# Splitting the opening load of a prefix-sum kernel between two DMA queues

## The chip, the core and the metric

The kernel runs on one core of one Trainium2 chip. Five engines work side by side, each with its own instruction stream: TensorE (PE, matrix products), VectorE (DVE), ScalarE (ACT), GpSimd (POOL) and SyncE (SP). Data comes from the device memory (HBM) into the on-chip SBUF of 128 partitions by DMA. Three of the engines issue DMAs here: SP and ACT into hardware queues, POOL into a software queue that can also convert float32 to bfloat16 on the way. All queues are served by the core's 16 DMA engines.

The metric is device time in microseconds (us); less is better. Beside it stands the profile of one execution, whose span is the time between its first and last instruction.

## The reference

The input x has 4 batches of 4224 x 4224 float32 numbers. For each batch the reference takes the two-dimensional prefix sum, reads its diagonal, and sums that up once more:

```
ps = np.cumsum(np.cumsum(x, axis=1), axis=2)
diag = np.diagonal(ps, axis1=1, axis2=2)
return np.cumsum(diag, axis=1).astype(np.float32)
```

The output is 4 x 4224. Every input element has to be read once: 4 x 4224 x 4224 x 4 bytes = 285.5 MB.

## The kernel before

The step from one diagonal element of the prefix sum to the next is the sum of a column's part above the diagonal and of a row's part up to the diagonal. So the kernel needs, for each index, one column sum and one row sum, and then two running sums.

The rows of a batch are read in strips of 768 rows (5 a batch and a rest of 384; the last batch is cut finer). A strip lies in SBUF as 128 partitions x 6 rows x 4224 columns in bfloat16: partition p holds the six neighbouring rows 6p to 6p+5. For the columns to the right of the diagonal block, TensorE adds up the rows with a selector matrix into `d` (lines 219 and 226). In the diagonal block DVE multiplies with a mask (line 361, `mu`), takes that part away (362), and the rest is summed along the rows by ACT (261, `dump`) and DVE (266, `acc`). `rowed` is another sum of DVE for TensorE. At the end of each batch two scans make the running sums.

The strips come from a pool of three buffers. The order of the instructions is as written (a manual schedule), and each engine takes its own in that order. POOL issues nearly all loads (line 71, `load_rows`, and line 87 for the first strip), each as soon as a buffer is free and POOL has come to it.

The change is at the very start. The first strip is loaded in two ways at once. Its first row of each partition (row 6p for partition p, 16,896 bytes each) goes in float32 by SP's queue into a third buffer that is seen as float32, `opening` (lines 77 and 78); ACT converts it into the strip when it has landed (line 89). The other five rows of each partition are loaded by POOL with conversion in two parts (line 87), and after them POOL issues the second strip (line 88, recorded at line 71). SP's queue then gets `head`, a load of 528 columns of the last batch's rows as 256 pieces of 2,112 bytes (line 83). These are used much later, but DVE's first instruction is their row sum (line 93), and what DVE makes after it, the selector (96, 97) and the masks of ones (102), is what TensorE's first product and POOL's mask instructions (103 and on) wait for. POOL makes masks and constants, and only then comes the load of the third strip (line 71), which takes the buffer that `opening` had.

At the end SP's queue carries the stores of the results (552 to 577), among them `whole_sums` from 11 partitions and `last_sums` from 10, both in pieces of 1,536 bytes.

Of the kernel before, what the change touches and what calls it, by code (L numbers as in the profile page):

```python
# [17 lines left out]
def kernel(  # L18
# [14 lines left out]
    nc = tc.nc  # L33
# [32 lines left out]
    def strip_tile():  # L66
        return strips.tile([P, F2, N], BF16, name="strip")
# [7 lines left out]

    src_0 = x[0, : F2 * P, :].rearrange("(p f) w -> p f w", f=F2)
    opening = strip_tile()[:, 0:2].rearrange("p f w -> p (f w)").bitcast(FP32)
    nc.sync.dma_start(out=opening, in_=src_0[:, 0])

    HC = 528  # L80
    src_a = x[LB, T0:TB, :].rearrange("(h p) w -> p h w", p=P)
# [17 lines left out]
    def upper_mask(f):  # L99
# [22 lines left out]
        out=um1,  # L122
        in_=um1,
# [10 lines left out]
        out=ident,  # L134
        in_=ident,
# [32 lines left out]
    def between_groups(name, turned):  # L168
# [27 lines left out]
        out=weights,  # L196
        in_=weights,
# [12 lines left out]
        out=steps, in_=steps, scalar=2, op=ALU.arith_shift_right  # L210
# [112 lines left out]
    for b in range(B):  # L323
# [86 lines left out]
        for h in range(2):  # L410
# [3 lines left out]
                out=r6[ps, k : k + 2 * ns : 2, :], in_=a6[ps, :, :, 1]  # L414
# [27 lines left out]
        if not whole:  # L442
# [9 lines left out]
            for sb, c0, c1 in (  # L452
# [8 lines left out]
                    out=part_b[:, sb, c0:c1],  # L461
                    in_=x[b, r0 : r0 + R, :TB].rearrange("r (k c) -> r k c", k=4)[
                        :, :, c0:c1
                    ],
# [29 lines left out]
        for i, (to, src) in enumerate(((c1, d), (c2, c1))):  # L494
            nc.vector.tensor_tensor_scan(  # L495
                out=to,
# [52 lines left out]
        for i in (1, 0):  # L549
# [3 lines left out]
            out=out[b, T0 : T0 + M0].unsqueeze(0), in_=yl[:, :M0]  # L553
        )
        nc.sync.dma_start(
            out=out[:LB, :].rearrange("b (g i) -> g b i", i=GW), in_=whole_sums
        )
        nc.sync.dma_start(
            out=out[b, :T0].rearrange("(g i) -> g i", i=GW), in_=last_sums[1:NG]
# [3 lines left out]
        for i in (1, 0):  # L563
# [8 lines left out]
            out=out[b, T0 + M0 : T0 + E0].unsqueeze(0), in_=yl[:, M0:E0]  # L572
# [35 lines left out]
```

## Time and profile before

| what | before |
|---|---|
| median of 3 runs | 667.43 us (667.42 to 667.55) |
| profiled execution's own time | 667.36 us |
| its span | 665.6 us |
| DMA traffic | 7810 packets, 144.31 MB written, mean 217 GB/s |
| HBM read | 285.47 MB, with what is written 429 GB/s over the span |
| busy: PE, DVE, ACT, POOL | 32%, 57%, 21%, 5% of the span |
| opening load (SP, 2112 KB) | 12.3 us from issue to landing |
| head load (SP, 528 KB) | 38.9 us |
| first strip by POOL (2112 KB and 3168 KB as written) | 17.2 us and 32.3 us |
| whole strips by POOL (6336 KB as written) | 65.5 us, median of 18 |

The page has a line for each engine over the span in 40 equal slices: a digit is the busy share in tenths, and 9 is 90% or more. The DMA line is the mean share of the 16 DMA engines. POOL's loads write half the bytes that they read, since they convert to two-byte numbers. A line of the order of events gives the start, the time of one instruction or group, engine and line, what it does, and in brackets how long the engine was idle before it and what ended that. In a line by stretches, each engine has its busy time and its instructions, in the order PE, PE's weight loads, DVE, ACT, POOL; then come TensorE's granted clock, the DMA share and GB/s. Beside the views, the trace has a record of each DMA packet, with its queue, start, duration and size; a packet of 4 bytes on a data queue is the completion mark of a transfer on one DMA engine.

### The profile page before, as it was taken

The numbers are of one execution on the slowest core, as the hardware profiler recorded it, in microseconds if no ns is written. First come the engines' busy times: TensorE is split into PE (matmuls) and PEld (weight loads), VectorE is DVE, ScalarE is ACT, GpSimd is POOL, SyncE is SP. The second block draws the span as 40 slices with busy tenths as digits, with TensorE's granted clock in tenths as the row PEclk, the third lists the DMA queues.
The fourth block names the chain that finished last, engine by engine and source line by source line (L and its number), as shares of the span: only waits on it lengthen the run. The fifth ranks groups of instructions, "written<-read, shape, count | busy, mean of one in ns | idle before, by whom it ended". The sixth has DMA issues, their size and how long they took to land.

```text
span 665.6 us, 2565 instructions
## 1 busy us (share of the span) xinstructions
PE 214.9 (32%) x979; PEld 97.5 (15%) x980; DVE 379.8 (57%) x176; ACT 139.1 (21%) x220; POOL 31.6 (5%) x60
## 2 busy tenths in 40 slices
PE   0044522403118143140311723404031354340468
PEld 0021211100003021010000311201000121120123
DVE  0045938476946173756794526456589433362866
ACT  2001121406300103040630020304063002030433
POOL 1014000000000000000000000000000000001000
PEclk9996757556558585665655858667555595775768
DMA  9999999999999999999999999999999999999998
GB/s 256 223 227 219 219 219 219 213 207 215 219 219 218 219 220 219 218 218 213 210 218 219 217 216 219 219 219 214 218 213 215 220 213 219 218 219 218 218 204 162
DMA packets 7810, 144.31 MB, mean 217 GB/s; under 512 B 714, under 2 KB 1014, under 8 KB 2166
## 3 DMA queue, kind: packets, MB, share of 16 engines
q0 software_dynamic: 7312, 141.39, 99.2%
q1 hardware_dynamic: 486, 2.77, 1.2%
q8 instruction: 7, 0.11, 0.1%
q14 instruction: 5, 0.04, 0.0%
HBM read 285.47 MB, written 0.07 MB: 429 GB/s over the span
## 4 chain that ended last, share of the span: by engine, by line
DVE 47%; another core or an unknown queue 30%; DMA 18%; POOL 2%; issue 1%; PE 1%; DVEq 0%; SPq 0%; POOLq 0%
DVE acc L266 25%; DMA strip<-in_x_dram 12%; DVE rowed L266 7%; DVE mu L361 7%; DVE strip L362 7%; DMA head<-in_x_dram 6%; POOL um L103 1%; PE d L219 1%; DVE um L102 1%; DVE c L495 0%; DVE whole_sums L495 0%; POOL strip L460 0%; DVE pu L266 0%; DVE whole_sums L287 0%
## 5 line engine op out<-in xcount | busy, mean ns | idle before, releaser
L261 ACT ACTIVATE dump<-strip 128x416 bf16<-128x416 bf16 (+6 forms) x108 | 123.6, 1145 | 505.4 <-DMA strip<-in_x_dram 502.7
L266 DVE TENSOR_REDUCE acc<-strip 128x6 f32<-128x4608 bf16 (+6 forms) x23 | 195.9, 8518 | 0.4
L361 DVE TENSOR_TENSOR mu<-strip,um 128x4608 bf16<-128x4608 bf16 (+1 forms) x24 | 52.4, 2183 | 221.1 <-DMA strip<-in_x_dram 221.0
L226 PEld LDWEIGHTS <-sel 128*11 128x11 bf16 x643 | 66.5, 103 | 435.8 <-issue 406.1
L219 PE MATMUL d<-strip,sel 128*11 128x384 bf16 x90 | 36.5, 406 | 281.0 <-DMA strip<-in_x_dram 239.4
L226 PE MATMUL d<-strip,sel 128*11 128x384 bf16 x441 | 113.6, 400 | 0.0
L219 PE MATMUL d<-mu,sel 128*11 128x384 bf16 x43 | 16.6, 386 | 117.6 <-DVE mu L361 117.5
L362 DVE TENSOR_TENSOR strip<-strip,mu 128x4608 bf16<-128x4608 bf16 (+1 forms) x24 | 52.4, 2183 | 1.0
L266 DVE TENSOR_REDUCE rowed<-strip 128x384 f32<-128x2304 bf16 x12 | 48.8, 4067 | 0.0
L226 PE MATMUL d<-mu,sel 128*11 128x384 bf16 x200 | 48.0, 377 | 0.0
L71 POOL DMA_DIRECT2D strip<-in_x_dram x23 | 15.7, 681 | 500.7 <-DVE acc L266 268.2
L93 DVE TENSOR_REDUCE hs<-head 128x2 f32<-128x1056 f32 x1 | 1.3, 1253 | 40.2 <-DMA head<-in_x_dram 40.2
L219 PEld LDWEIGHTS <-sel 128*11 128x11 bf16 x134 | 13.6, 102 | 60.4 <-DVE sel L97 41.6
L219 PE MATMUL d<-rowed,sel_f 128*11 128x384 f32 x24 | 12.6, 616 | 25.3 <-DVE rowed L266 25.3
L261 ACT ACTIVATION_READ_ACCUMULATOR dump<-strip 128x1 f32 x108 | 20.1, 186 | 0.0
L219 PE MATMUL d<-ident,rows 128*11 128x128 f32 x24 | 5.2, 378 | 16.8 <-DVE rows L422 16.8
L219 PE MATMUL fold<-um,ident_h 128*128 128x512 bf16 x27 | 8.1, 475 | 0.3 <-issue 0.3
L103 POOL TENSOR_SCALAR_AFFINE_SELECT um<-um 128x4608 bf16<-128x4608 bf16 (+1 forms) x2 | 5.2, 2610 | 43.4 <-DVE um L102 43.4
L89 ACT CAST strip<-strip 128x4224 bf16<-128x4224 f32 x1 | 3.7, 3711 | 11.1 <-DMA strip<-in_x_dram 11.1
L219 PEld LDWEIGHTS d<-rowed,sel_f 128*11 128x11 f32 x24 | 1.4, 93 | 30.1 <-DVE rowed L266 30.0
L266 DVE TENSOR_REDUCE pu<-d 11x1 f32<-11x384 f32 x4 | 2.2, 546 | 6.2 <-PE d L219 6.2
L102 DVE MEMSET um<- 128x4608 bf16 (+1 forms) x2 | 4.9, 2458 | 1.1 <-issue 1.1
(108 smaller groups left out, 77.3 us busy)
## 6 DMA issues: line engine op xcount, KB each, us to landing
strip<-in_x_dram POOLq DMA_DIRECT2D x18, 6336.0 KB, 65.5
strip<-in_x_dram POOLq DMA_DIRECT2D x6, 3168.0 KB, 55.8
strip<-in_x_dram SPq DMA_DIRECT2D x1, 2112.0 KB, 12.3
strip<-in_x_dram POOLq DMA_DIRECT2D x1, 2112.0 KB, 17.2
strip<-in_x_dram POOLq DMA_DIRECT2D x1, 1080.0 KB, 49.9
strip<-in_x_dram POOLq DMA_DIRECT2D x1, 768.0 KB, 52.9
strip<-in_x_dram POOLq DMA_DIRECT2D x3, 256.0 KB, 54.1
head<-in_x_dram SPq DMA_DIRECT2D x1, 528.0 KB, 38.9
```

What stands on the lines that cost most here:

```text
L71: nc.gpsimd.dma_start(out=o, in_=x[b, r0 : r0 + f * P, :].rearrange("(p f) w -> p f w", f=f))
L89: nc.scalar.copy(out=prefetched[0][:, 0], in_=opening)
L93: nc.vector.reduce_sum(out=hs[:, 0:2], in_=head, axis=AX.X)
L102: nc.vector.memset(um, 1.0)
L103: nc.gpsimd.affine_select(out=um, in_=um, compare_op=ALU.is_gt, fill=0.0, base=0, pattern=[[-1, f], [1, f * P]], channel_multiplier=-f,)
L219: nc.tensor.matmul(o, lhsT=lhsT, rhs=rhs, start=start, stop=False, skip_group_check=True)
L226: te.add_instruction(mybir.InstMatmult(start_tensor_calc=False, stop_tensor_calc=False, tile_position=(0, 0), tile_size=(P, P if lhsT.shap ...
L261: nc.scalar.activation(out=dump[:, :w], in_=src, func=ACT.Copy, accum_out=acc)
L266: nc.vector.reduce_sum(out=acc, in_=src, axis=AX.X)
L361: nc.vector.tensor_mul(out=mu, in0=block, in1=um)
L362: nc.vector.tensor_sub(out=block, in0=block, in1=mu)
```

## The change

The load into `opening` is issued as two DMAs. The 16 partitions from 0 to 15 go by ACT's queue, the 112 from 16 to 127 by SP's. Bytes, source and destination are the same. On SP the head load follows, as before; on ACT the conversion of line 89 is the next instruction, and it now waits for both.

```diff
     src_0 = x[0, : F2 * P, :].rearrange("(p f) w -> p f w", f=F2)
     opening = strip_tile()[:, 0:2].rearrange("p f w -> p (f w)").bitcast(FP32)
-    nc.sync.dma_start(out=opening, in_=src_0[:, 0])
+    nc.scalar.dma_start(out=opening[:16], in_=src_0[:16, 0])
+    nc.sync.dma_start(out=opening[16:], in_=src_0[16:, 0])
```

## The prediction

> **What bounds the kernel now.** I read the page's slices first, then its DMA queues, then busy time by stretches, then the chain of waits and the order of events in the first 60 us.
>
> ```profile
> DVE  0045938476946173756794526456589433362866
> ...
> DMA  9999999999999999999999999999999999999998
> ...
> q0 software_dynamic: 7312, 141.39, 99.2%
> q1 hardware_dynamic: 486, 2.77, 1.2%
> ```
>
> In the slices, the DMA line is a 9 in all but the last, while the busiest engine, DVE, is half idle. Of the time of the 16 DMA engines, 99.2% is POOL's queue (q0), which loads the strips; the hardware queue (q1), with the opening load in it, has 1.2%. So I asked for the stretches; the second to last figure of a line is the DMA share.
>
> ```profile
> 1.90:6.00 4.10, 0.00 (x0) 0.00 (x0) 0.00 (x0) 0.20 (x1) 1.36 (x3) 1.00 1.10 371
> 6.00:14.00 8.00, 0.00 (x0) 0.00 (x0) 0.00 (x0) 0.82 (x1) 0.00 (x0) 1.00 0.99 261
> 14.00:58.00 44.00, 10.78 (x54) 5.26 (x55) 8.43 (x14) 2.89 (x1) 10.66 (x24) 0.97 1.00 220
> ...
> 600.00:662.30 62.30, 31.42 (x149) 13.61 (x150) 37.35 (x30) 19.05 (x29) 4.13 (x7) 0.70 1.00 210
> 662.30:665.60 3.30, 0.84 (x10) 0.35 (x8) 0.88 (x5) 0.71 (x3) 0.00 (x0) 1.00 0.14 21
> ```
>
> The DMA engines work without a hole from 1.9 us to 662.3 us, and 3.3 us of tail follow. A microsecond that a DMA engine loses at the start is therefore a microsecond at the end: nothing later is idle and could take it up. The chain of waits names DVE and unknown queues for much of the span, but that chain runs beside a stream that is never dry. The chain and the order of events matter only for whether the next load is always issued in time:
>
> ```profile
> 0.81 1.28 ACT L89 ACT_TABLE_LOAD   x1 [0.81 <-PEq L592]
> 0.82 0.41 SPq L78 DMA_DIRECT2D strip<-in_x_dram  x1
> 1.28 0.42 SPq L83 DMA_DIRECT2D head<-in_x_dram  x1
> 1.33 1.22 POOL L87 DMA_DIRECT2D strip<-in_x_dram  x2 [0.81 <-POOLq L592]
> ...
> 13.18 3.71 ACT L89 CAST strip<-strip 128x4224 bf16<-128x4224 f32 x1 [11.09 <-DMA strip<-in_x_dram]
> 40.17 1.25 DVE L93 TENSOR_REDUCE hs<-head 128x2 f32<-128x1056 f32 x1 [40.17 <-DMA head<-in_x_dram]
> ...
> 57.00 0.79 POOL L71 DMA_DIRECT2D strip<-in_x_dram  x1
> ```
>
> ACT does nothing until the opening has landed. DVE waits for the head load until 40.17, POOL's masks wait for DVE, and the load of the third strip stands behind those masks on POOL and goes out at 57.00.
>
> **The change, part by part.** The packet records of the trace show the opening as 128 packets of 16,896 bytes, one a row, 8 on each of 16 engines. The first of each engine took 1.16 us on average, the second 0.65; alone on its engine a packet then takes 0.629 us. POOL's first packet starts at 5.54, after five rows of each engine; from there SP's and POOL's packets take turns, with POOL's at 1.264 us, later 1.886.
>
> *SP's issue* shrinks to 112 rows; its row is 0.41 us, of which I save nothing, since the first packet starts at 1.85 either way. *ACT's issue* is new: about 0.41 us by SP's row, and the table load of 1.28 us may stand before it. Either order puts it on the queue by 2.5 us, when only the opening is moving. Hidden by ACT's idle time until 13.18; without that cover it would cost 0.41 us. *The cast* now waits for two loads. Behind it on ACT stands nothing until 64.47 (the row sums of strip 1), and its reader, TensorE, waits for DVE's selector until 41.63 in any case: 16.9 to 41.6 is 24.7 us of cover. *More completion packets*: 16, one an engine, of 0.022 us: +0.02 us. *Around the span*: 667.36 - 665.6 = 1.76 us; another queue in use might change it, nothing bounds that but that SP's queue is in it already: 0.
>
> *How the rows are dealt out.* At the end of the kernel the trace shows small stores: one of 11 partitions, one of 10, three of one partition. They leave 11 + 10 + 3 = 24 completion packets: a load or store of few partitions puts one row on one engine each. So ACT's 16 rows should be one row on each of the 16 engines and SP's 112 rows seven on each: in packets every engine keeps its eight, and by count the sum is zero. No row of the trace shows a transfer of 112.
>
> *Whether a row then takes as long as before* is the whole question, because 16 engines now all move rows of partitions 0 to 15. The nearest row is those stores. Their packets of 1,536 bytes from partitions 0 to 10 gather around levels, with others between: 65 ns twice, a bunch at 113 to 119, one at 165 to 181, one at 219 to 240. That is about 1 : 1.8 : 2.6 : 3.5, as if up to four engines that touch one group of four partitions shared one engine's rate. The 128-row opening shows none of that, all its later packets at 0.629 to 0.66.
>
> ACT's part: 16 rows in four groups of four partitions, four engines in each. At the level of 3.5, a row takes 2.2 us instead of 0.629: +1.60 us on every engine. Ends: 0, if the writing side doesn't share as the reading side of the stores does, and +1.89 at a full fourfold. I take 1.60, the nearest in partitions.
>
> The Trainium skill, "SBUF — State Buffer", section "Door 1: The DMA port swizzle", speaks against the change: partitions 0 to 15 reach four of 16 ports, measured there at 104 GB/s. By that figure, as an estimate, the 270,336 bytes take 2.6 us where a sixteenth of the opening took 0.63, so the part would cost 1.97 us instead of 1.60 and the total would be 0.37 us higher.
>
> SP's part: seven rows an engine. The 128-row opening shows that 16 engines run undisturbed when each has its own eight partitions. 112 partitions are 14 such sets, for 16 engines: some must share. Ends: 0, by the opening's own packets, and all seven rows at the two-sharers level, 7 x 0.629 x (115/65 - 1) = +3.39 us. If the rows fall on the sets by chance, an engine finds one of the 15 others in its set with 1 - (13/14)^15 = 0.67; I take 0.67 x 3.39 = +2.27 us.
>
> *The head load* follows on SP's queue, 16 packets an engine in turn with POOL's. If the opening is slow, fewer of its rows are done when POOL's packets begin at 5.5, and each row left over puts one more POOL packet (1.886 us) ahead of the head's last, beyond the delay of the whole stream. One or two rows: DVE, POOL's masks and the third strip's issue are 1.9 to 3.8 us later against the stream. What covers it: strip 1's last packets end at 63.73 to 64.11, the issue is at 57.00, and POOL's first issue took 5.54 - 1.33 = 4.2 us to its first packet, so 63.7 - 57.0 - 4.2 = 2.5 us. I cost it at 0, with an end of 3.8 - 2.5 = +1.3.
>
> Sum against the profiled execution: 667.36 + 0.02 + 1.60 + 2.27 = 671.25; the median of the runs is 0.07 above the profiled one: 671.3 us.
>
> **The rivals.**
>
> *The packets don't disturb each other* (chance 0.21). For it: every engine keeps eight rows, and the levels of the stores are of reading SBUF and writing HBM, not of the opposite. Against it: the bunches at 1.8, 2.6 and 3.5 are too regular for chance. Time: 667.43 + 0.02 = 667.45; if only part of ACT's cost arises, up to 668.7.
>
> *Two queues help at the start* (chance 0.04 of a gain over 0.2%). The first packets lose 1.16 - 0.63 = 0.53 us an engine; with a row of another queue beside it an engine might fill this. For it: the row exists. Against it: even all of it gives 666.9, a change of 0.08%, and the head, which could come a packet earlier, holds up nothing as the stream is never dry. It would have to save over 1.33 us before the first POOL packet, which nothing in the rows offers. This is the case that ends not slower, together with the one before.
>
> *The third strip comes late* (chance 0.13). The mechanism of the head load, decisive from 2.5 us of delay against the stream. For it: POOL's chain from 40.17 to 57.00 has no slack of its own. Against it: it needs a slow opening first. With two leftover rows 671.3 + 1.3 = 672.6; with three, (5.7 - 2.5) = 3.2 more, 674.5.
>
> *Only ACT's rows are slow* (within the forecast's case): 667.43 + 1.60 = 669.0. With both upper ends and no late strip: 667.43 + 1.89 + 3.39 = 672.7.
>
> **How the numbers follow.** The forecast's case, with one or both parts slow and the third strip in time, has 0.62: 671.3, from 669.0 to 672.7. The late strip has 0.13, undisturbed 0.21, faster 0.04. A measurement of this kernel tells about 0.2% (1.33 us) from no change. Slower: 0.62 + 0.13 = 0.75, of which I move 0.02 to the middle for parts that come out small: 0.73. Within: 0.23. Faster: 0.04. To leave out no more than 2 in 10 the range goes down to the undisturbed case, 667.2, and up to 674.2, short of three leftover rows.
>
> **What would show it.** In the packet records of the changed kernel: ACT's 16 packets at 2 us or more, SP's 112 partly at 1.1 us instead of 0.629, none of POOL's changed (1.264 and 1.886). The cast starts at 16 to 20 us instead of 13.18; the head lands at 45 us or later instead of 40.17; the DMA share stays at 1.00 up to the end, which lies about 4 us later. The third strip's issue moves with the head, and a DMA share below 1.00 near 65 to 72 us would be the late strip. I am wrong if the 16,896-byte packets keep 0.629, or if they are slow and the stream makes up for it, which would need idle DMA time that I have not seen.

## The result, and the profile after

The changed kernel takes 670.11 us (median of 6 runs, 669.74 to 670.46) against 667.42 us: 2.69 us more, ratio 1.0038 (95% interval 1.0028 to 1.0049). The forecast was 671.3 us, its range 667.2 to 674.2. One execution of all that follow, 689.9 us in the run with the 112 rows and the moved bytes, was in a slower state and is left out. The profiled execution took 670.14 us with a span of 668.4 us; before it was 667.36 and 665.6.

The page of the changed kernel, its slices and its DMA queues (q10 is ScalarE's queue):

```profile
DMA  9999999999999999999999999999999999999998
...
q0 software_dynamic: 7312, 141.39, 98.7%
q1 hardware_dynamic: 470, 2.50, 1.3%
q10 hardware_dynamic: 32, 0.27, 0.2%
```

The DMA line is as full as before and POOL's queue has the same packets. What grew is the share of the two hardware queues, from 1.2% to 1.5%, with the same bytes. ScalarE's 32 packets are 16 rows and 16 completion marks, one mark for each DMA engine, so each of the 16 rows went to an engine of its own.

The stretches of the changed kernel (columns as before, the DMA share and GB/s last):

```profile
1.90:6.00 4.10, 0.00 (x0) 0.00 (x0) 0.00 (x0) 0.00 (x0) 1.36 (x3) 1.00 0.97 194
...
600.00:665.10 65.10, 31.84 (x151) 13.80 (x151) 40.17 (x30) 19.05 (x29) 4.14 (x7) 0.71 1.00 209
665.10:668.40 3.30, 0.80 (x10) 0.32 (x8) 0.88 (x5) 0.71 (x3) 0.00 (x0) 1.00 0.14 21
```

This is the whole change in two numbers: from 1.9 to 6 us the engines are all but fully busy (0.97) and yet move 194 GB/s instead of 371. (The view counts a whole packet where it starts, which is how the kernel before comes to a share of 1.10. With packets cut at the borders, the records give 188 GB/s instead of 343, and a share of 0.96 instead of 0.97.) The tail is still 3.3 us, and in between nothing is idle, so what the first microseconds lose moves the end from 662.3 to 665.1.

The order of events at the start of the changed kernel:

```profile
0.81 0.41 ACTq L78 DMA_DIRECT2D strip<-in_x_dram  x1
0.82 0.38 SPq L79 DMA_DIRECT2D strip<-in_x_dram  x1
1.25 0.42 SPq L84 DMA_DIRECT2D head<-in_x_dram  x1
...
16.24 1.28 ACT L90 ACT_TABLE_LOAD   x1 [16.24 <-DMA strip<-in_x_dram]
17.53 3.71 ACT L90 CAST strip<-strip 128x4224 bf16<-128x4224 f32 x1
43.28 1.25 DVE L94 TENSOR_REDUCE hs<-head 128x2 f32<-128x1056 f32 x1 [43.28 <-DMA head<-in_x_dram]
...
60.12 0.79 POOL L71 DMA_DIRECT2D strip<-in_x_dram  x1
```

Both issues leave at once. The table load, which stood ahead of the wait before, now stands behind it; the conversion ends at 21.2 us, and its reader still waits for DVE until 44.7. DVE's start and the third strip's issue are each 3.1 us later.

The packet records say which packets got slower. The opening's packets, sorted by start and taken in groups of 16 (about one an engine), with the mean time in us:

```
place          1     2     3     4     5     6     7     8
before       1.16  0.65  0.63  0.63  0.64  0.64  0.64  0.64
changed      1.25  1.28  1.62  0.94  0.93  0.78  0.65  0.66
```

The changed kernel's sum is 8.12 us an engine instead of 5.64 (sums of the unrounded records), +2.47 us. Places 2 and 3, where ScalarE's rows and the SyncE rows that follow them stand, have +1.62 of it: ScalarE's 16 rows took 1.28 us on average, the SyncE rows after them 1.62. The records have no row's partition, so they don't say by themselves on which partitions engines met. POOL's packets keep 1.264 and 1.886 us. The engines also come apart: the second strip's completion marks end between 66.03 and 67.18, before between 63.75 and 64.13. The slowest engine sets the end: POOL's last 16 packets end within 0.40 us of each other, before within 0.21, and the last one 2.76 us later, where the mean engine lost 2.47.

### The profile page after: what moved, and what is told of

Same layout as the page of the kernel before. It is cut to its first block, busy times and chain, and to the rows that moved or that the text cites. A ratio compares the mean times of both kernels' runs of the same rounds, so it can differ in the third digit from the quotient of the medians.

```text
span 668.4 us, 2568 instructions
## 1 busy us (share of the span) xinstructions
PE 214.9 (32%) x979; PEld 97.7 (15%) x980; DVE 380.0 (57%) x176; ACT 139.1 (21%) x220; POOL 31.6 (5%) x60
## 4 chain that ended last, share of the span: by engine, by line
DVE 47%; another core or an unknown queue 30%; DMA 18%; POOL 2%; issue 1%; PE 1%; DVEq 0%; SPq 0%; POOLq 0%
DVE acc L267 25%; DMA strip<-in_x_dram 12%; DVE rowed L267 7%; DVE mu L362 6%; DVE strip L363 6%; DMA head<-in_x_dram 6%; POOL um L104 1%; PE d L220 1%; DVE um L103 1%; DVE c L496 0%; DVE whole_sums L496 0%; POOL strip L461 0%; DVE pu L267 0%; DVE whole_sums L288 0%
## 5 line engine op out<-in xcount | busy, mean ns | idle before, releaser
L220 PEld LDWEIGHTS <-sel 128*11 128x11 bf16 x134 | 13.8, 103 | 63.6 <-DVE sel L98 44.7
L220 PE MATMUL d<-halves,rows 128*11 128x64 f32 x48 | 5.3, 289 | 0.0
## 6 DMA issues: line engine op xcount, KB each, us to landing
strip<-in_x_dram SPq DMA_DIRECT2D x1, 1848.0 KB, 15.3
```

The costliest lines, as they stand in the source:

```text
L220: nc.tensor.matmul(o, lhsT=lhsT, rhs=rhs, start=start, stop=False, skip_group_check=True)
```

## The experiments

Three theories stood at the start. Theory 1: engines that write into the same group of partitions share one engine's rate. Theory 2: a second hardware queue costs the time. Theory 3: the rows are read from HBM in an unlucky order. Differences below are against the runs of the kernel before on the same chip, 667.41 to 667.49 us.

**One queue.** Both parts on SyncE's queue:

```diff
-    nc.scalar.dma_start(out=opening[:16], in_=src_0[:16, 0])
+    nc.sync.dma_start(out=opening[:16], in_=src_0[:16, 0])
     nc.sync.dma_start(out=opening[16:], in_=src_0[16:, 0])
```

> Both parts are issued by SyncE's queue, the 16 partitions first; ScalarE issues nothing. Theory 1 (engines that write the same group of partitions share one engine's rate): the loss stays, 1.5 to 3.5 us over before (669 to 671), and the 16 packets of the first part take about 2 us. Theory 2 (a second hardware queue costs the time): gone, 667.4. Theory 3 (the rows are read from HBM in an unlucky order): the loss stays, about 2.7 us.

669.76 us (669.60 to 669.88), +2.33, ratio 1.0033 (1.0021 to 1.0046). The packets of the eight places: 1.28, 1.67, 1.00, 0.97, 0.84, 0.69, 0.68, 0.65. Without the second queue most of the loss is still there; theory 2 cannot explain it. One expectation failed: the 16 rows, here in the first place, took 1.28 us and not about 2 (the first place before: 1.16). The rows after them took 1.67. It looks as if a row's recorded time also had what the row ahead of it left behind; that is a reading, and no run tests it.

**Cut by columns.** Two queues, but all 128 partitions in each:

```diff
-    nc.scalar.dma_start(out=opening[:16], in_=src_0[:16, 0])
-    nc.sync.dma_start(out=opening[16:], in_=src_0[16:, 0])
+    nc.scalar.dma_start(out=opening[:, :528], in_=src_0[:, 0, :528])
+    nc.sync.dma_start(out=opening[:, 528:], in_=src_0[:, 0, 528:])
```

> Two queues as in the change, but cut by columns: ScalarE's queue takes columns 0 to 527 of all 128 partitions, SyncE's the other 3696. Theory 1: no loss, 667.2 to 667.9, packets of SyncE's queue near 0.55 us (14,784 bytes at the opening's rate). Theory 2: the loss of 2.7 us stays, 670. Theory 3: no loss.

667.47 us (667.40 to 667.56), +0.04, ratio 0.9999 (0.9990 to 1.0008). The DMA queues and issues of this kernel (size in KB, us from issue to landing):

```profile
q1 hardware_dynamic: 486, 2.50, 1.0%
q10 hardware_dynamic: 144, 0.27, 0.2%
...
strip<-in_x_dram SPq DMA_DIRECT2D x1, 1848.0 KB, 12.5
...
strip<-in_x_dram ACTq DMA_DIRECT2D x1, 264.0 KB, 9.4
```

The changed kernel has the same bytes on the same two queues:

```profile
strip<-in_x_dram SPq DMA_DIRECT2D x1, 1848.0 KB, 15.3
...
strip<-in_x_dram ACTq DMA_DIRECT2D x1, 264.0 KB, 6.8
```

SyncE's part lands in 12.5 us by columns, where it took 15.3. From the third place on, its packets take 0.55 to 0.57 us for 14,784 bytes, the rate of 16,896 bytes in 0.63 to 0.64. Two queues cost nothing here, and bring nothing.

**An extra load, four ways.** The opening stays whole on SyncE, and ScalarE's queue loads 270,336 bytes more into a place that nothing reads (two rows of the third buffer that are free at that time). The first lines are common to all:

```diff
-    opening = strip_tile()[:, 0:2].rearrange("p f w -> p (f w)").bitcast(FP32)
+    third = strip_tile()
+    opening = third[:, 0:2].rearrange("p f w -> p (f w)").bitcast(FP32)
+    spare = third[:, 2:4].rearrange("p f w -> p (f w)").bitcast(FP32)
+    nc.scalar.dma_start(out=spare[:16], in_=src_0[:16, 0])            # partitions 0 to 15
+    nc.scalar.dma_start(out=spare[:, :528], in_=src_0[:, 0, :528])    # all 128
+    nc.scalar.dma_start(out=spare[::8], in_=src_0[:16, 0])            # 0, 8 ... 120
+    nc.scalar.dma_start(out=spare[:112:7], in_=src_0[:16, 0])         # 0, 7 ... 105
     nc.sync.dma_start(out=opening, in_=src_0[:, 0])
```

Each kernel has one of the four. Partitions 0 to 15:

> The opening as before by SyncE, and an extra load by ScalarE's queue: the first rows of 16 partitions once more, into partitions 0 to 15 of a spare place that nothing reads. 16 packets of 16,896 bytes are 0.64 us more on each DMA engine. Theory 1: 0.64 + 1.6 = 2.2 us over before (up to 2.5), 669.6. Theory 2: the same as the extra load into 128 partitions. Theory 3: like theory 1 if these rows are the unlucky ones.

All 128 partitions:

> The opening as before by SyncE, and an extra load of the same 270,336 bytes by ScalarE's queue into all 128 partitions (528 columns each, 2,112 bytes a packet, eight packets of about 0.09 us an engine). Theory 1: only its own time, 0.7 to 0.8 us over before, 668.2. Theory 2: as much as the extra load into 16 partitions, over 2 us.

Every eighth, and every seventh:

> The extra load of 16 rows as in the run that puts them into partitions 0 to 15, same queue, same source rows, same packets, but into partitions 0, 8, 16 ... 120. Theory 1 with groups of four neighbouring partitions alone: only its own time, 0.64 us over before, 668.1. Theory 1 with sets of eight partitions as the Trainium skill, SBUF - State Buffer, Door 1, maps them (two of the 16 rows in each of eight sets): some 0.6 us more, 668.7 (an estimate from that map). Theory 3 (the source rows): as in the other run, 3.1 us, 670.5.

> The same extra load into partitions 0, 7, 14 ... 105. By the groups of four no two rows meet, and by the map of the skill's page only two pairs do: 0.64 to 0.9 us over before, 668.1 to 668.3, and less than with every eighth partition if the map holds. Theory 3: 3.1 us, 670.5.

| extra load into | median, us | over before | ratio (95%) | its 16 packets, us |
|---|---|---|---|---|
| partitions 0 to 15 | 670.53 | +3.10 | 1.0046 (1.0034 to 1.0059) | 0.67 to 2.21 |
| all 128 | 668.19 | +0.76 | 1.0012 (1.0003 to 1.0020) | 128 of 0.086 (median) |
| every eighth | 668.35 | +0.86 | 1.0010 (1.0001 to 1.0019) | 0.63 to 0.97 |
| every seventh | 668.19 | +0.70 | 1.0008 (0.9999 to 1.0017) | 0.63 to 0.81 |

Same queue, and in three of the four the same source rows and packet sizes: where the rows are written makes 2.2 to 2.4 us of difference. Theory 3 falls with that, since the source is the same. With 0.64 us for the packets themselves, 16 rows in neighbouring partitions cost 2.46 us extra, more than the 1.6 to 1.9 expected. In that run the packets of the nine places take 1.29, 1.45, 1.96, 0.81 and then 0.63 to 0.64: of the opening's rows it is mainly the one after ScalarE's that suffers, the next has 0.81, and from the fifth place on they are undisturbed.

One thing was not equal: the spread rows came later, at 5.5 to 6.0 us, the others at 3.0 to 3.6.

**The 16 partitions, later.** In the program ScalarE makes a small copy before it issues:

```diff
+    early = consts.tile([P, 2, 8], FP32, name="early")
+    nc.vector.memset(early[:, 0], 0.0)
+    nc.scalar.copy(out=early[:, 1], in_=early[:, 0])
     nc.sync.dma_start(out=opening, in_=src_0[:, 0])
     nc.scalar.dma_start(out=spare[:16], in_=src_0[:16, 0])
```

> The extra load of 16 rows into partitions 0 to 15 again, but issued after a small copy on ScalarE (with its table load before it), so that its packets come at 4 to 6 us, as those into every eighth or seventh partition did (5.5 to 6.0 us), and not at 3.0 us. If the partitions decide: 2 to 3 us over before, 669.4 to 670.4. If it was the early arrival in the start-up that cost the time: 0.65 to 0.9 us, 668.1 to 668.3, as with the spread partitions.

669.96 us (669.78 to 671.10), +2.55, ratio 1.0039 (1.0025 to 1.0053). The copy didn't hold the issue back: the trace has the issue at 0.99 us, before the copy at 2.10. Still the packets start later, at 3.6 to 4.3 us, after a second place that took 0.68 (0.65 in the kernel before), and they and the next take 1.28 and 1.72. They lie some 1.7 us ahead of the spread ones, so this run alone doesn't close the gap. The run with the 16 rows last, below, does: there they come at 12.6 us, after the time of the spread ones, and are slow all the same. So it is not the start-up; the partitions decide. Less 0.64, this is 1.9 us for the 16 rows.

**The other part alone.** First with the bytes of the 16 rows moved to all 128 partitions of the spare place:

```diff
-    nc.scalar.dma_start(out=opening[:16], in_=src_0[:16, 0])
+    nc.vector.memset(opening[:16], 0.0)
+    nc.scalar.dma_start(out=spare[:, :528], in_=src_0[:, 0, :528])
     nc.sync.dma_start(out=opening[16:], in_=src_0[16:, 0])
```

> Left out: the first rows of partitions 0 to 15, which VectorE sets to zero instead. SyncE loads the 112 rows as in the change; ScalarE's queue moves the bytes of the 16 rows into all 128 partitions of a spare place. So the 112 rows are alone. By the prediction's term they cost 2.27 us, 669.8 with 0.1 for the smaller packets. If the 16 rows are the whole loss: 667.6. The changed kernel's packets let me expect something between, 0.3 to 1.0 us, 667.9 to 668.5.

669.77 us (median of six, 669.28 to 671.31), +2.28, ratio 1.0030 (1.0018 to 1.0042). That is more than I expected from the changed kernel's packets, and the prediction's own term, 2.27. But the small packets beside the rows were slow too (0.133 us in the median, up to 0.415, instead of 0.086), and the profiled execution is 1.5 us above the median. So once more without them:

```diff
     nc.vector.memset(opening[:16], 0.0)
-    nc.scalar.dma_start(out=spare[:, :528], in_=src_0[:, 0, :528])
     nc.sync.dma_start(out=opening[16:], in_=src_0[16:, 0])
```

> Left out: the first rows of partitions 0 to 15, which VectorE sets to zero, and now also the load of their bytes elsewhere. SyncE loads the 112 rows, ScalarE issues nothing. Each engine has one packet of 0.64 us less, so without any sharing the time would be 666.8. If the 112 rows cost 1.3 to 1.4 us, as their packets say in the run with the 16 rows last: 668.1. If they cost 2.2 us, as in the run that moved the 16 rows' bytes into a spare place beside them: 669.0, and the sum of both parts is simply not reached in the changed kernel.

668.11 us (667.69 to 668.78), +0.68, ratio 1.0008 (0.9999 to 1.0017), with 0.64 us less to move: the 112 rows by themselves cost 1.32 us (0.57 to 1.77 by the interval, so below 2.27). Seven places: 1.18, 0.77, 1.07, 0.88, 0.89, 0.66, 0.64. With the small packets beside them the last two were 1.04 and 1.02; why those made it about a microsecond worse was not tried further. One rival stays for this part: 112 rows are also read from HBM in another order than 128 (theory 3), and no run separates that from where they are written.

**Do the parts add up?** One queue, the 16 rows last:

```diff
+    nc.sync.dma_start(out=opening[16:], in_=src_0[16:, 0])
+    nc.sync.dma_start(out=opening[:16], in_=src_0[:16, 0])
-    nc.scalar.dma_start(out=opening[:16], in_=src_0[:16, 0])
-    nc.sync.dma_start(out=opening[16:], in_=src_0[16:, 0])
```

> One queue (SyncE), first the 112 rows and then the 16, so that the 16 rows come between POOL's packets at about 12 us and not in the first microseconds. If the costs of the two parts add up once they lie apart in time: 2.2 for the 112 rows and about 1.6 to 1.9 for the 16, 3.8 to 4.1 us over before, 671.3 to 671.6, the 16 packets at 1.5 us and more. If POOL's packets between the rows hide the sharing of the 16: 2.2 to 2.5 us, 669.7 to 669.9.

670.20 us (669.91 to 670.41), +2.79, ratio 1.0038 (1.0026 to 1.0051): between the two expectations. The 16 rows now run at 12.6 to 13.8 us and take 1.33 on average, and POOL's 16 packets that start from 13.3 take 1.96 instead of 1.264. That is +0.69 and +0.69, 1.4 us for the 16 rows, which POOL's packets don't hide. Places 1 to 7, the 112 rows, are 1.4 us over the kernel before. Apart in time the two costs do add up, by this run's one profile; they are both smaller than the expectation had them.

**Halves.** A split that leaves each engine four rows of each half:

```diff
-    nc.scalar.dma_start(out=opening[:16], in_=src_0[:16, 0])
-    nc.sync.dma_start(out=opening[16:], in_=src_0[16:, 0])
+    nc.scalar.dma_start(out=opening[:64], in_=src_0[:64, 0])
+    nc.sync.dma_start(out=opening[64:], in_=src_0[64:, 0])
```

> The opening cut in the middle: partitions 0 to 63 by ScalarE's queue, 64 to 127 by SyncE's, four rows an engine each. Theory 1: engines share in pairs if the two halves lie on separate sets as the skill's map has it, and a row takes up to twice 0.63 until POOL's packets come in between: 1 to 4 us over before, 668.4 to 671.4. With groups of four neighbouring partitions alone four rows of one engine are one group: no loss, 667.4.

671.18 us (671.14 to 671.28), +3.69, ratio 1.0051 (1.0038 to 1.0064). The places: 1.35, 1.16, 1.33, 1.33, 1.13, 0.78, 0.76, 0.84. The start in this run's stretches:

```profile
1.90:8.00 6.10, 0.00 (x0) 0.00 (x0) 0.00 (x0) 0.00 (x0) 1.35 (x3) 1.00 1.04 222
```

All 16 engines busy, but at 222 GB/s (again counted by a packet's start; with packets cut at the borders 197, and 323 before). The kernel before has this:

```profile
1.90:8.00 6.10, 0.00 (x0) 0.00 (x0) 0.00 (x0) 0.20 (x1) 1.36 (x3) 1.00 1.05 338
```

The two halves didn't run side by side: SyncE's rows fill the first four places, and ScalarE's first row comes at 7.06 us. In places 3 and 4, where only SyncE's half is moving, a row takes 1.33 us, 2.1 times 0.63: half the partitions, half the rate. Groups of four neighbouring partitions alone can't give this if the four rows of an engine are neighbours, because each engine would then have a group for itself; the records don't show which rows an engine got. The Trainium skill, "SBUF — State Buffer", section "Door 1: The DMA port swizzle", has it: 64 partitions from 64 on reach eight of the 16 ports. The trace agrees with that here. With every eighth partition the same map would put two rows on each of eight ports and give, as an estimate, about 1.26 us if they run at the same moment; the packets took 0.63 to 0.97, 0.80 on average, so this run doesn't show it. Every seventh cost 0.16 us less than every eighth, the way the map has it, but the two intervals overlap. For the 16 rows it is shown that the partitions decide; for the 112 and for the halves it is the reading that fits. What exactly the engines share isn't shown.

## Why the prediction was right, and where it was off

- *The DMA stream never runs dry, so a loss at the start is a loss at the end.* Right. The packets lost 2.47 us, the last load landed 2.76 us later (662.31 to 665.07), the profiled execution took 2.78 more.
- *ACT's issue, the second wait, the completion marks at nothing.* Right. The column split has all three and is within 0.04 us of before.
- *One row an engine for the 16, seven for the 112.* The 16 marks on ScalarE's queue show the first; the second was not read directly.
- *The opening's later packets at 0.629 to 0.66.* Nearly: two of them took 0.72 and 0.73, which changes nothing in the sum.
- *ACT's part, +1.60.* About right in size, with some luck, since the level of 3.5 came from stores, which read SBUF. Places 2 and 3 of the changed kernel have +1.62, but that isn't ACT's part alone: the 112 rows by themselves have +0.12 and +0.44 in these places. By difference of the runs, 2.69 - 1.32 = 1.37 us are left for it. I put it into ScalarE's own packets, at 2 us or more, and that failed: they took 1.28 on average, 1.95 at most, and the SyncE rows after them 1.62. Alone the part cost 1.4 us by the packets of one run, and 1.9 and 2.46 by the times of two others, whose intervals overlap. The Trainium skill, "SBUF — State Buffer", section "Door 1: The DMA port swizzle", would by its 104 GB/s for 16 partitions have had 1.97 as an estimate, in between.
- *SP's part, +2.27.* This is the term that was mis-sized. It was two thirds of a loss of 3.39, which takes seven rows at the two-sharers level of 1.11 us. The part alone cost 1.32 us (changed kernel: places 1 and 4 to 8 together +0.85). The slowed rows took 0.77 to 1.07 us, and they were only the four after the first; the last two took 0.64 to 0.66, once POOL's packets stood between. I had let the sharing go on for two thirds of all seven. With small packets beside it the loss was 2.28, with the last two rows slow as well, so its size depends on what runs beside it. That POOL's packets leave room because they write half as many bytes in their time is an argument and was not tested; the 16 rows in four groups slowed even them.
- *The sum.* 1.60 + 2.27 gave 3.87; measured were 2.69. Of the 1.18 too much, SP's term has 0.95 and ACT's 0.23. The range reached from no change to +6.8 us, so that the time lies in it says little; the packets and the experiments carry the mechanism.
- *The head and the third strip.* I took the head's landing to be 45 us or later, because fewer rows would be done when POOL's packets begin at 5.5 us. They didn't begin at 5.5. The first started at 7.67, when 64 of the opening's 128 rows were done and 80 begun; before it was the same 64 and 80, at 5.54. So nothing extra stood ahead of the head, which landed at 43.28, 3.1 us later, and the third strip's issue at 60.12 came in time: from 58 to 75 us the packets fill the 16 engines' time as fully as before. The late-strip rival didn't occur. The cover is less sure than it looks: by the prediction's way 66.0 - 60.1 - 4.2 = 1.7 us were left, but the 4.2 us from issue to first packet were 6.3 at the start of the changed kernel.
- *Undisturbed packets, and two queues that help at the start.* Both refuted, by the packets and by the column split.

## What to carry to other kernels

In a kernel whose DMA engines are never idle, read a change of a load by the DMA time that its packets take, not by when it is issued: waits, queues and issues hardly mattered here (0.3 us of a late start in the halves), but packets that took longer for the same bytes did. If a load is to be cut, cut it along its free dimension, with all 128 partitions in each piece, as the column split did at no cost; pieces of 16, 64 and 112 partitions lost time, by the account above because DMA engines met on the same partitions. Here 270 KB into 16 neighbouring partitions cost 1.4 to 2.5 us beyond its own time, and the same bytes over 128 partitions about a tenth of a microsecond.

## What the runs showed that I had not expected

POOL's first packet doesn't come at a fixed time after its issue, but, in these kernels, after five rows of the hardware queues on each engine (80 begun in all): at 5.54 us before, 7.67 in the changed kernel, 8.24 with the halves, though POOL issued at 1.32 to 1.33 in all three. With the extra rows spread over every eighth and seventh partition it was six (96 begun, 6.28 and 6.14 us). Where small packets run beside the rows, the count differs.

Some forms of the load are issued more slowly. With the destination stepping over partitions, ScalarE's issue took 0.57 and 0.61 us instead of 0.41, and its first packet came at 5.5 to 5.7 us, in the sixth place, where that of the contiguous one came at 3.0, in the second. The order of events, of the run with every eighth partition:

```profile
0.81 0.57 ACTq L80 DMA_DIRECT2D strip<-in_x_dram  x1
```

The halves show it too, without a step:

```profile
0.81 0.56 ACTq L78 DMA_DIRECT2D strip<-in_x_dram  x1
0.81 0.55 SPq L79 DMA_DIRECT2D strip<-in_x_dram  x1
```

SyncE's first packet came at 2.15 us instead of 1.85, so some 0.3 us of the 3.69 are not sharing; ScalarE's came only at 7.06, in the fifth place.

None of these kernels beats the one before. The column split, which spreads the issue over two queues without the loss, only equals it.
